# Long convolutions of a hybrid encoder layer: two stages of a 16-point transform as sums inside the matrix products

## The chip, the cores and the metric

One core of a Trainium2 chip runs the whole layer as one program. The metric is the device time of that program in microseconds (us); lower is better. Before the change three runs gave 3840.48, 3847.14 and 3849.62 us, median 3847.14 us.

## The reference, cut to what matters

The layer has four token mixers side by side. The one that the change touches is the Hyena mixer, two long convolutions over 2048 tokens in 256 channels:

```
def fft_long_conv(u, h_freq, skip):
    l = u.shape[1]
    uf = jnp.fft.rfft(u, n=2 * l, axis=1)
    y = jnp.fft.irfft(uf * h_freq[None], n=2 * l, axis=1)[:, :l]
    return y + u * skip

def hyena_mixer(z, ...):
    v, x1, x2 = jnp.split(short_conv(z, ...), 3, axis=-1)
    y = x1 * fft_long_conv(v, hf[:, 0], s[0])
    y = x2 * fft_long_conv(y, hf[:, 1], s[1])
```

Beside it stand a state space mixer and two softmax attentions with four heads each; then an output projection, a feed-forward part and a gated embedding. All is float32.

## The kernel before, in words

**The convolution.** Each long convolution is computed by `long_conv` (L1210) for half of the channels (128) at a time: two halves `hh`, two orders, so four calls, one after the other. The 2048 tokens are 128 rows (partitions) by 16 time residues t. A transform over the tokens is a 128-point part, done as matrix products with the tables `c_dft_f` and `c_dft_i`, and a 16-point part over t, done as two rounds of 4-point transforms with element-wise instructions. A 4-point transform (`Dft16.four`) is `first` (two instructions over 128x512: sums and differences, L1022 and L1023) and `last` (two over 128x256 and four over 128x128, L1028 to L1033). `rotate` multiplies by twiddle factors (nine ScalarE copies with a scale and one addition).

One call goes through three stages:

- Forward: for b = 0 to 3, two groups (a) of four products of 128 columns each into one PSUM tile (L1221), one ScalarE copy of it into `h_z` (L1223), then `four` from `h_z` over `h_s` back to `h_z`, then `rotate`.
- Middle: for ka = 0 to 3, `four`, the product with the filter's spectrum `h_sp`, the inverse `four`, `rotate`. No TensorE work.
- Inverse: for b = 0 to 3, the inverse `four` from `h_s` over `h_z` back to `h_s`, then eight products of 128 columns (L1255) into one PSUM tile, then one VectorE product with the gate (L1258).

The instructions of b (or ka) = 0 and 2 run on GpSimd (POOL), those of 1 and 3 on VectorE (DVE), by the list `ENG[1]`.

**What runs beside it.** `hyena_main` is a background generator: `Background.advance` is called once for each of the twelve steps of an attention unit (64 units, one for each head and 128 queries) and takes from the generator as many pieces as its costs (the numbers in `yield`) allow. So the four calls lie inside the attention, whose units need TensorE for scores (L447), transposes (L491) and weighted sums (L501), VectorE for moving each score block out of PSUM (L450, L452), ScalarE for exponentials (L457) and for moving transposes out (L496). The next generator in the queue forms the operands of the output projection (`out_weights`), in memory that the convolutions have left. The final order on each engine is written by a planner that simulates the program; the priority of background pieces is raised by 150 instructions. Each engine then takes its list in order.

Of the kernel before, what the change touches and what calls it, by code (L numbers as in the profile page):

```python
# [11 lines left out]
F32 = mybir.dt.float32  # L12
# [3 lines left out]
AF = mybir.ActivationFunctionType  # L16
# [1183 lines left out]
def hyena_main(ops, const, A, S, cp, wk, ps_pool):  # L1200

    tc, nc = ops.tc, ops.nc
    dft = Dft16(ops, wk, 128, [nc.vector if e else nc.gpsimd for e in ENG[1]])

    def mats(src, which):
        f = wk.tile([128, 2, 2, 128], F32, name="h_mat", bufs=4)
        nc.sync.dma_start(f, src[:, which, 0:2])
        return f

    def long_conv(u, order, hh, gate, dst):  # L1210
        z = wk.tile([128, 2, 16, 128], F32, name="h_z", bufs=1)
        s = wk.tile([128, 2, 16, 128], F32, name="h_s", bufs=1)
        for b in range(4):
            eng = dft.engines[b]
            zc, sc = z[:, :, b::4], s[:, :, b::4]
            for a in range(2):
                f = mats(A["c_dft_f"], slice(b + 4 * a, None, 8))
                ps = ps_pool.tile([128, 512], F32, name="ps_hy", tag="ps_hy").rearrange("p (t r c) -> p t r c", t=2, r=2)
                for i in range(2):
                    for r in range(2):  # L1220
                        nc.tensor.matmul(ps[:, i, r], lhsT=f[:, i, r], rhs=u[:, b + 4 * a + 8 * i], start=i + r == 0,  # L1221
                                         stop=True, skip_group_check=True)
                nc.scalar.activation(zc[:, :, a::2].rearrange("p r t c -> p t r c"), ps, AF.Copy)  # L1223
                yield 1.7
            yield from dft.four(eng, zc, sc, False)
            if b:
                dft.rotate(eng, zc, sc, b, False)
                yield 1.6
        for ka in range(4):
            eng = dft.engines[ka]  # L1230
            zc, sc = z[:, :, ts(ka, 4)], s[:, :, ts(ka, 4)]
            sp = wk.tile([128, 2, 4, 128], F32, name="h_sp", bufs=2)
            nc.sync.dma_start(sp, S["hspec"][order, hh, :, ka])
            yield from dft.four(eng, zc, sc, False)
            for r in range(2):
                eng.tensor_tensor(sc[:, r], zc[:, r], sp[:, 0], ALU.mult)
            for r in range(2):
                eng.tensor_tensor(zc[:, r], zc[:, r], sp[:, 1], ALU.mult)
            yield 2.2
            eng.tensor_tensor(sc[:, 0], sc[:, 0], zc[:, 1], ALU.subtract)  # L1240
            eng.tensor_tensor(sc[:, 1], sc[:, 1], zc[:, 0], ALU.add)
            yield 1.1
            yield from dft.four(eng, sc, zc, True)
            if ka:
                dft.rotate(eng, sc, zc, ka, True)
                yield 1.6
        for b in range(4):
            zc, sc = z[:, :, b::4], s[:, :, b::4]
            yield from dft.four(dft.engines[b], sc, zc, True)
            ps = ps_pool.tile([128, 4, 128], F32, name="ps_hy", tag="ps_hy")  # L1250
            for a in range(2):
                f = mats(A["c_dft_i"], slice(b + 8 * a, b + 8 * a + 5, 4))
                for i in range(2):
                    for r in range(2):
                        nc.tensor.matmul(ps[:, 2 * a + i], lhsT=f[:, i, r], rhs=sc[:, r, 2 * a + i],  # L1255
                                         start=a + i + r == 0, stop=r == 1, skip_group_check=True)
                yield 1.7
            nc.vector.tensor_mul(dst[:, b::4], ps, gate[:, b::4])  # L1258
            yield 0.6

    for hh in range(2):
        v, x1, x2 = (wk.tile([128, 16, 128], F32, name=n, bufs=1) for n in ("hy_v", "hy_x1", "hy_x2"))
        for j, d in enumerate((v, x1, x2)):
            nc.sync.dma_start(d, S["hyc"][2 * j + hh])
        yield from long_conv(v, 0, hh, x1, v)
        yield from long_conv(v, 1, hh, x2, x1)
        nc.sync.dma_start(S["yhs"].rearrange("(p t) c -> p t c", t=16)[:, :, ts(hh, 128)], x1)
        yield 0.0

# [374 lines left out]
C, S, T, W = "combine", "scale", "transpose", "weigh"  # L1644
# [39 lines left out]
def tile_hybrid_encoder(ctx, tc, A, out):  # L1684
# [28 lines left out]
    with ExitStack() as ac:  # L1713
# [21 lines left out]
        bg.add(together(background(s5_setup, "ss_c", "ss_w", "right"), hyena_conv, "hc_c", "hc_w", EMN[1]))  # L1735
        bg.add(together(background(s5_main, "sm_c", "sm_w", "right"), embedding, "em_c", "em_w", EMN[0]))
        bg.add(background(hyena_main, "hm_c", "hm_w", "right"))
        bg.add(out_weights)
        ip.run(const, bg.advance, lambda: bg.until(4))
# [100 lines left out]
```

## Time and profile before

| | |
|---|---|
| median of three runs | 3847.14 us |
| the profiled execution's own time | 3846.66 us |
| its span in the profile | 3844.9 us |
| mean granted TensorE clock | 0.953 of full |
| attention, first to last score or sum | 558.8 to about 1996 us |
| the four long convolutions | 1310 to 1882 us |

The span is the time from the first to the last instruction of the profiled execution; times of rows below count from its start. Engines are PE (TensorE products), PEld (TensorE weight loads, beside PE), DVE (VectorE), ACT (ScalarE), POOL (GpSimd), SP (which issues DMAs). "Busy" is the time in which an engine had at least one instruction in execution; for PE the ends are modelled and consecutive products overlap.

### The profile page before, as it was taken

The numbers are of one execution on the slowest core, as the hardware profiler recorded it, in microseconds if no ns is written. First come the engines' busy times: TensorE is split into PE (matmuls) and PEld (weight loads), VectorE is DVE, ScalarE is ACT, GpSimd is POOL, SyncE is SP. The second block draws the span as 40 slices with busy tenths as digits, with TensorE's granted clock in tenths as the row PEclk, the third lists the DMA queues.
The fourth block names the chain that finished last, engine by engine and source line by source line (L and its number), as shares of the span: only waits on it lengthen the run. The fifth ranks groups of instructions, "written<-read, shape, count | busy, mean of one in ns | idle before, by whom it ended". The sixth has DMA issues, their size and how long they took to land. (4 is left out here: it accounts for less than half of the span.)

```text
span 3844.9 us, 55782 instructions
## 1 busy us (share of the span) xinstructions
PE 3504.9 (91%) x19814; PEld 2782.5 (72%) x19814; DVE 2678.9 (70%) x5382; ACT 1802.5 (47%) x3089; POOL 1869.3 (49%) x1735
## 2 busy tenths in 40 slices
PE   8999988998999977877889979999999998989887
PEld 6889876676777756665667768887788876767666
DVE  6657538777565698798767774447554577777877
ACT  5334316666666655655664443334333343333344
POOL 1333003671663587677546554445444444344454
PEclk9999999999999988988899989999999999999998
DMA  4544652226223412421244452223322244445644
GB/s 145 181 142 162 221 164 50 104 90 194 91 93 98 153 37 83 121 56 55 85 160 154 149 164 77 88 78 99 102 88 79 85 162 168 172 153 170 210 165 151
DMA packets 350998, 480.45 MB, mean 125 GB/s; under 512 B 57307, under 2 KB 257759, under 8 KB 346207
## 3 DMA queue, kind: packets, MB, share of 16 engines
q1 hardware_dynamic: 276672, 369.13, 31.0%
q10 hardware_dynamic: 74048, 107.76, 7.9%
q8 instruction: 156, 2.56, 0.3%
q14 instruction: 122, 1.00, 0.1%
HBM read 313.46 MB, written 167.53 MB: 125 GB/s over the span
## 5 line engine op out<-in xcount | busy, mean ns | idle before, releaser
L447 PE MATMUL ps_s<-k_sb,q_sb 96*128 96x512 f32 x1280 | 483.9, 466 | 109.9 <-DVE four_s L452 51.1
L457 ACT ACTIVATE at_s<-at_s,least_s 128x2048 f32<-128x2048 f32 x192 | 383.8, 2000 | 133.1 <-DVE least_s L456 127.5
L817 PE MATMUL ps_st<-t_hi,s_hi 128*128 128x512 f32 x984 | 398.5, 406 | 49.3 <-DVE st_sum L844 24.0
L452 DVE CUSTOM_DVE_ANT_0 at_s<-ps_s,strip 128x512 f32<-128x512 f32 x512 | 340.1, 684 | 126.1 <-PE ps_s L447 102.4
L817 PE MATMUL ps_st<-t_lo,s_hi 128*128 128x512 f32 x984 | 395.4, 402 | 17.0 <-DVE t_lo L41 17.0
L496 ACT ACTIVATE at<-ps_at 128x512 f32<-128x512 f32 x512 | 292.0, 593 | 231.9 <-PE ps_at L491 197.6
L817 PE MATMUL ps_st<-t_hi,s_lo 128*128 128x512 f32 x984 | 393.8, 401 | 5.6 <-DVE s_lo L41 5.6
L447 PEld LDWEIGHTS ps_s<-k_sb,q_sb 96*128 96x128 f32 x1280 | 233.8, 202 | 206.6 <-DVE four_s L452 77.9
L40 ACT ACTIVATE s_hi<-s_raw 128x512 fp32r<-128x512 f32 (+1 forms) x336 | 207.4, 618 | 357.9 <-PE ps_st L817 283.3
L501 PE MATMUL ps_o<-at,v_sb 128*64 128x128 f32 x4096 | 352.9, 296 | 11.2 <-DVE o_sb L518 4.8
L491 PE MATMUL ps_at<-ident,at_s 128*128 128x128 f32 x2048 | 325.5, 293 | 39.4 <-ACT at L496 23.9
L41 DVE TENSOR_TENSOR s_lo<-s_raw,s_hi 128x512 fp32r<-128x512 f32 (+1 forms) x336 | 265.8, 793 | 133.4 <-ACT s_hi L40 133.2
L501 PEld LDWEIGHTS ps_o<-at,v_sb 128*64 128x64 f32 x4096 | 256.8, 145 | 111.5 <-issue 91.7
L40 ACT ACTIVATE a_hi<-a_raw 128x512 fp32r<-128x512 f32 (+1 forms) x252 | 155.2, 618 | 379.8 <-PE ps_st L817 212.4
L491 PEld LDWEIGHTS ps_at<-ident,at_s 128*128 128x128 f32 x2048 | 258.5, 150 | 100.5 <-ACT at L496 33.0
L801 POOL TENSOR_TENSOR s_raw<-a_raw 128x512 f32<-128x512 f32 (+1 forms) x84 | 113.6, 1352 | 441.1 <-DMA a_raw<-in_w_up_dram 136.1
L817 PE MATMUL ps_st<-b_hi,a_hi 128*128 128x512 f32 x656 | 263.1, 401 | 34.8 <-ACT b_hi L40 15.6
L41 DVE TENSOR_TENSOR a_lo<-a_raw,a_hi 128x512 fp32r<-128x512 f32 (+1 forms) x252 | 232.5, 924 | 76.0 <-ACT a_hi L40 75.0
L471 POOL TENSOR_SCALAR at_s<-at_s,f 128x1024 f32<-128x1024 f32 (+1 forms) x48 | 74.7, 1556 | 424.1 <-DMA q_sb<-d_qmr 193.0
L817 PEld LDWEIGHTS ps_st<-t_hi,s_hi 128*128 128x128 f32 x984 | 191.5, 195 | 102.1 <-DVE st_sum L844 28.3
L817 PE MATMUL ps_st<-b_lo,a_hi 128*128 128x512 f32 x656 | 260.8, 398 | 4.5 <-DVE b_lo L41 3.1
L817 PE MATMUL ps_st<-b_hi,a_lo 128*128 128x512 f32 x656 | 259.4, 396 | 0.0
(521 smaller groups left out, 8883.1 us busy)
## 6 DMA issues: line engine op xcount, KB each, us to landing
d_h<-st_row ACTq DMA_DIRECT2D x64, 512.0 KB, 3.3
st_row<-d_h SPq DMA_DIRECT2D x64, 512.0 KB, 4.4
a_raw<-in_w_gate_dram SPq DMA_DIRECT2D x44, 512.0 KB, 4.1
a_raw<-in_w_up_dram SPq DMA_DIRECT2D x44, 512.0 KB, 3.9
d_g<-st_row ACTq DMA_DIRECT2D x44, 512.0 KB, 3.9
f_mat<-in_c_dft_f_dram SPq DMA_DIRECT2D x32, 512.0 KB, 4.1
a_raw<-d_g SPq DMA_DIRECT2D x32, 512.0 KB, 4.9
w_raw<-in_w_in_dram SPq DMA_DIRECT2D x48, 256.0 KB, 3.4
```

What stands on the lines that cost most here:

```text
L40: nc.scalar.activation(hi, src, AF.Copy)
L41: nc.vector.tensor_sub(lo, src, hi.bitcast(F32))
L447: nc.tensor.matmul(ps, lhsT=lhs, rhs=rhs[:, ts(c, 512)], start=n == 0, stop=n == len(products) - 1)
L452: nc.vector.tensor_tensor_reduce(dst, ps, at.strip[:, ds(1920 - 128 * self.t + 512 * c, 512)], self.slope, 3e38, ALU.add, ALU.min, least)
L457: nc.scalar.activation(s, s, AF.Exp, bias=least, scale=-1.0, accum_out=self.total[name])
L471: nc.gpsimd.tensor_scalar(s2[:, n:], s2[:, n:], f, 0.0, ALU.mult, ALU.add)
L491: nc.tensor.transpose(ps[:, j], src[:, ts(4 * g + j, 128)], at.ident)
L496: nc.scalar.activation(tile, ps, AF.Copy)
L501: mm = lambda out, lhsT, rhs, first, last: nc.tensor.matmul(out, lhsT=lhsT, rhs=rhs, start=first, stop=last, skip_group_check=True)
L801: eng.tensor_add(s1, a21, a22)
L817: nc.tensor.matmul(bank, lhsT=l[x][:, c], rhs=r[y], start=first and c + k == 0, stop=c == kb - 1 and k == 2, skip_group_check=True)
```

## The change

In the forward stage `first` goes away. Its sums and differences of the parts t and t + 8 are made in PSUM: for each table the product with u[t] is written to both halves of the tile (a broadcast operand, 256 columns), and the product with u[t + 8] and with its negative (256 columns, from a tile that holds u[8:16] a second time with its sign turned, at index 16 to 23) is added. The ScalarE copy puts the tile into `h_s` and `last` follows.

In the inverse stage `last` goes away. `first` stays; a ScalarE copy makes the negatives of the odd parts, and each of the four outputs of the 4-point transform is accumulated from two operands for each table: sixteen products of 128 columns in place of eight.

The negated copy of the input is made by ScalarE: once for each half of the channels over 128x1024, and in the first order's inverse stage once for each b over 128x256. The input tile `hy_v` grows from 16 to 24 parts, and the costs in `yield` change.

```diff
-                for i in range(2):
-                    for r in range(2):
-                        nc.tensor.matmul(ps[:, i, r], lhsT=f[:, i, r], rhs=u[:, b + 4 * a + 8 * i], start=i + r == 0,
-                                         stop=True, skip_group_check=True)
-                nc.scalar.activation(zc[:, :, a::2].rearrange("p r t c -> p t r c"), ps, AF.Copy)
-                yield 1.7
-            yield from dft.four(eng, zc, sc, False)
+                for r in range(2):
+                    mm(ps[:, :, r], lhsT=f[:, 0, r], rhs=u[:, t][:, None, :].to_broadcast([128, 2, 128]), start=r == 0,
+                       stop=False, skip_group_check=True)
+                    mm(ps[:, :, r], lhsT=f[:, 1, r], rhs=u[:, t + 8 :: 8], start=False, stop=True, skip_group_check=True)
+                nc.scalar.activation(sc[:, :, a::2].rearrange("p r t c -> p t r c"), ps, AF.Copy)
+                yield 2.4
+            dft.last(eng, zc, sc, False)
+            yield 2.2
...
-            yield from dft.four(dft.engines[b], sc, zc, True)
+            dft.first(dft.engines[b], zc, sc[:, :, 0:2], sc[:, :, 2:4])
+            neg = sc[:, :, 0:2]
+            nc.scalar.activation(neg, zc[:, :, 1::2], AF.Copy, scale=-1.0)
+            yield 2.2
+            re, im, rn, jn = zc[:, 0], zc[:, 1], neg[:, 0], neg[:, 1]
+            terms = (((re[:, 0], re[:, 1]), (im[:, 0], im[:, 1])), ((re[:, 2], jn[:, 1]), (im[:, 2], re[:, 3])),
+                     ((re[:, 0], rn[:, 0]), (im[:, 0], jn[:, 0])), ((re[:, 2], im[:, 3]), (im[:, 2], rn[:, 1])))
...
-                        nc.tensor.matmul(ps[:, 2 * a + i], lhsT=f[:, i, r], rhs=sc[:, r, 2 * a + i],
-                                         start=a + i + r == 0, stop=r == 1, skip_group_check=True)
-                yield 1.7
-            nc.vector.tensor_mul(dst[:, b::4], ps, gate[:, b::4])
+                        for k, x in enumerate(terms[2 * a + i][r]):
+                            mm(ps[:, 2 * a + i], lhsT=f[:, i, r], rhs=x, start=a + i + r + k == 0, stop=r + k == 2,
+                               skip_group_check=True)
+                yield 2.4
+            nc.vector.tensor_mul(dst[:, b:16:4], ps, gate[:, b:16:4])
+            if again:
+                nc.scalar.activation(dst[:, 16 + b :: 4], dst[:, 8 + b : 16 : 4], AF.Copy, scale=-1.0)
             yield 0.6
...
-            nc.sync.dma_start(d, S["hyc"][2 * j + hh])
-        yield from long_conv(v, 0, hh, x1, v)
-        yield from long_conv(v, 1, hh, x2, x1)
+            nc.sync.dma_start(d[:, 0:16], S["hyc"][2 * j + hh])
+        nc.scalar.activation(v[:, 16:24], v[:, 8:16], AF.Copy, scale=-1.0)
+        yield from long_conv(v, 0, hh, x1, v, True)
+        yield from long_conv(v, 1, hh, x2, x1, False)
```

## Rows read from the trace of the kernel before

**Rows 1.** The page: busy time of each engine over the span.

```profile
PE 3504.9 (91%) x19814; PEld 2782.5 (72%) x19814; DVE 2678.9 (70%) x5382; ACT 1802.5 (47%) x3089; POOL 1869.3 (49%) x1735
```

**Rows 2.** Windows by stage: stretch, length, busy time of engines, clock, DMA share, GB/s.

```profile
1324.00:1350.00 26.00, 24.64 (x209) 19.63 (x208) 20.88 (x53) 21.60 (x46) 22.70 (x24) 1.00 0.39 119
1350.00:1420.00 70.00, 48.38 (x286) 34.78 (x285) 69.79 (x134) 31.84 (x61) 60.26 (x55) 0.75 0.12 40
1420.00:1452.00 32.00, 29.80 (x229) 23.48 (x229) 27.57 (x64) 19.37 (x35) 22.61 (x22) 0.96 0.23 67
1452.00:1480.00 28.00, 25.75 (x202) 20.96 (x197) 19.62 (x57) 19.16 (x42) 22.99 (x25) 0.95 0.45 139
1480.00:1552.00 72.00, 51.68 (x348) 38.59 (x347) 68.52 (x134) 35.31 (x69) 55.99 (x54) 0.78 0.13 40
1552.00:1590.00 38.00, 35.07 (x254) 27.20 (x254) 31.45 (x77) 20.20 (x33) 25.05 (x24) 0.96 0.19 55
1590.00:1622.00 32.00, 29.31 (x244) 23.63 (x243) 24.72 (x63) 24.72 (x46) 21.03 (x22) 1.00 0.86 246
1622.00:1696.00 74.00, 52.14 (x316) 37.39 (x317) 70.41 (x132) 32.66 (x62) 58.75 (x54) 0.74 0.27 70
1696.00:1735.00 39.00, 37.09 (x307) 30.49 (x307) 35.22 (x94) 25.71 (x49) 26.49 (x28) 0.96 0.21 62
1735.00:1766.00 31.00, 31.00 (x264) 24.96 (x264) 23.72 (x71) 23.78 (x40) 19.78 (x18) 1.00 0.32 95
1766.00:1846.00 80.00, 54.83 (x347) 38.86 (x348) 75.17 (x150) 41.70 (x90) 71.34 (x70) 0.79 0.08 23
1846.00:1881.00 35.00, 31.87 (x251) 25.77 (x247) 29.40 (x70) 16.28 (x24) 16.98 (x16) 0.95 0.14 42
```

**Rows 3.** Windows: attention before and after the convolutions, same columns.

```profile
550.00:1310.00 760.00, 707.05 (x5105) 522.54 (x5104) 520.60 (x1421) 489.18 (x698) 371.78 (x428) 0.96 0.36 109
1885.00:2000.00 115.00, 100.01 (x800) 75.20 (x796) 78.11 (x205) 77.72 (x115) 55.65 (x55) 0.90 0.40 133
```

**Rows 4.** Groups, a middle stage (1766 to 1846): busy, mean ns | idle before, releasers.

```profile
L447 PE MATMUL ps_s<-k_sb,q_sb 96*128 96x512 f32 x61 | 27.3, 529 | 21.4 <-DVE four_s L452 13.9 <-DVE at_s L450 6.6 <-DMA q_sb<-d_qda 0.8
```

**Rows 5.** Groups, a forward stage (1735 to 1766), the same line.

```profile
L447 PE MATMUL ps_s<-k_sb,q_sb 96*128 96x512 f32 x36 | 12.8, 438 | 0.0
```

**Rows 6.** Tile h_mat: the convolutions' products, duration ns min/median/max, first and last start.

```profile
L1221 PE MATMUL ps_hy<-hy_v,h_mat x256: 272/275/377, 1324.1 to 1762.3; 128*128 128x128 f32 x128
L1255 PE MATMUL ps_hy<-h_s,h_mat x256: 272/275/582, 1431.8 to 1878.0; 128*128 128x128 f32 x128
```

**Rows 7.** Timeline of weight loads at 1335: start us, length us, count.

```profile
1334.90 1.86 PEld L1221 LDWEIGHTS ps_hy<-hy_v,h_mat 128*128 128x128 f32 x16
```

**Rows 8.** Timeline of PE at 1158: products of 256 columns.

```profile
1157.94 1.03 PE L1574 MATMUL ps_hy<-s5m_m,s5m_uT 128*128 128x256 f32 x4
1158.81 0.38 PE L1577 MATMUL ps_hy<-s5m_wout,s5m_xs 128*128 128x256 f32 x1
```

**Rows 9.** Groups of 1324 to 1880: VectorE and GpSimd instructions of the 4-point transforms.

```profile
L1022 DVE TENSOR_TENSOR h_s<-h_z 128x512 f32<-128x512 f32 x16 | 23.8, 1487 | 1.8 <-POOL h_s L1023 1.6
L1023 DVE TENSOR_TENSOR h_s<-h_z 128x512 f32<-128x512 f32 x16 | 19.2, 1199 | 0.0
L1028 DVE TENSOR_TENSOR h_s<-h_z 128x256 f32<-128x256 f32 x16 | 13.2, 824 | 0.0
L1033 DVE TENSOR_TENSOR h_s<-h_z 128x128 f32<-128x128 f32 x16 | 9.5, 595 | 0.0
L1022 POOL TENSOR_TENSOR h_s<-h_z 128x512 f32<-128x512 f32 x16 | 21.8, 1365 | 19.0 <-ACT h_z L1223 11.9 <-DVE h_z L1028 4.1 <-DVE h_z L1053 3.0
L1028 POOL TENSOR_TENSOR h_s<-h_z 128x256 f32<-128x256 f32 x16 | 17.2, 1074 | 0.2
```

**Rows 10.** Groups of 1324 to 1880: ScalarE copies of the convolutions.

```profile
L1223 ACT ACTIVATE h_z<-ps_hy 128x512 f32<-128x512 f32 x32 | 18.8, 593 | 14.2 <-PE ps_hy L1221 14.2
L1050 ACT ACTIVATE h_s<-h_z 128x256 f32<-128x256 f32 x36 | 13.6, 416 | 11.3 <-DVE h_z L1031 9.9 <-DVE h_z L1033 1.2
```

**Rows 11.** Groups of 1324 to 1880: the inverse stage's products.

```profile
L1255 PE MATMUL ps_hy<-h_s,h_mat 128*128 128x128 f32 x256 | 39.0, 289 | 5.2 <-DVE h_s L1032 3.8 <-DVE h_s L1028 1.4
```

More of the change, by code (lines that the diff above doesn't have):

```diff
@@ L1208, in mats, with long_conv @@
         return f
-    def long_conv(u, order, hh, gate, dst):
+    def long_conv(u, order, hh, gate, dst, again):
         z = wk.tile([128, 2, 16, 128], F32, name="h_z", bufs=1)
         s = wk.tile([128, 2, 16, 128], F32, name="h_s", bufs=1)
+        mm = nc.tensor.matmul
         for b in range(4):
@@ L1216, in long_conv @@
             for a in range(2):
-                f = mats(A["c_dft_f"], slice(b + 4 * a, None, 8))
+                t = b + 4 * a
+                f = mats(A["c_dft_f"], slice(t, None, 8))
                 ps = ps_pool.tile([128, 512], F32, name="ps_hy", tag="ps_hy").rearrange("p (t r c) -> p t r c", t=2, r=2)
-                for i in range(2):
-                    for r in range(2):
-                        nc.tensor.matmul(ps[:, i, r], lhsT=f[:, i, r], rhs=u[:, b + 4 * a + 8 * i], start=i + r == 0,
-                                         stop=True, skip_group_check=True)
-                nc.scalar.activation(zc[:, :, a::2].rearrange("p r t c -> p t r c"), ps, AF.Copy)
-                yield 1.7
-            yield from dft.four(eng, zc, sc, False)
+                for r in range(2):
[6 more added lines that the diff above has]
+            yield 2.2
             if b:
@@ L1254, in long_conv @@
                     for r in range(2):
-                        nc.tensor.matmul(ps[:, 2 * a + i], lhsT=f[:, i, r], rhs=sc[:, r, 2 * a + i],
-                                         start=a + i + r == 0, stop=r == 1, skip_group_check=True)
-                yield 1.7
-            nc.vector.tensor_mul(dst[:, b::4], ps, gate[:, b::4])
+                        for k, x in enumerate(terms[2 * a + i][r]):
[5 more added lines that the diff above has]
+                nc.scalar.activation(dst[:, 16 + b :: 4], dst[:, 8 + b : 16 : 4], AF.Copy, scale=-1.0)
             yield 0.6
     for hh in range(2):
-        v, x1, x2 = (wk.tile([128, 16, 128], F32, name=n, bufs=1) for n in ("hy_v", "hy_x1", "hy_x2"))
+        v, x1, x2 = (wk.tile([128, n, 128], F32, name=name, bufs=1) for name, n in (("hy_v", 24), ("hy_x1", 16), ("hy_x2", 16)))
         for j, d in enumerate((v, x1, x2)):
-            nc.sync.dma_start(d, S["hyc"][2 * j + hh])
-        yield from long_conv(v, 0, hh, x1, v)
-        yield from long_conv(v, 1, hh, x2, x1)
+            nc.sync.dma_start(d[:, 0:16], S["hyc"][2 * j + hh])
+        nc.scalar.activation(v[:, 16:24], v[:, 8:16], AF.Copy, scale=-1.0)
+        yield from long_conv(v, 0, hh, x1, v, True)
+        yield from long_conv(v, 1, hh, x2, x1, False)
         nc.sync.dma_start(S["yhs"].rearrange("(p t) c -> p t c", t=16)[:, :, ts(hh, 128)], x1)
```

## The prediction

> **What bounds the kernel now.** The page's first part puts TensorE ahead of all engines over the whole span, 91% busy against 70% for VectorE [rows 1]. That mean says nothing about the convolutions, so I went from the timeline of one call (which shows where its three stages lie) to the windows, one for each stage of each of the four calls [rows 2]. The reader is to see two kinds of row. The four middle stages (the windows of 70, 72, 74 and 80 us, 296 us together) have VectorE at 94 to 100% and TensorE at 69 to 72% with a clock of 0.74 to 0.79. The eight forward and inverse stages (26, 32, 28, 38, 32, 39, 31 and 35 us, 261 us together) have TensorE at 91 to 100% with a clock of 0.95 or more: its busy times add up to 244.5 us of 261, so 16.5 us are idle. VectorE has 212.6 us there (81%), ScalarE 170.8 (65%), GpSimd 177.6 (68%).
>
> The groups say the same by what ends the waits. In the last middle stage the score products waited 21.4 us, 20.5 of them for VectorE to empty a PSUM tile [rows 4]; in the forward stage just ahead of it, 0.0 us [rows 5]. So the limit changes from stage to stage, and the change takes VectorE and GpSimd work out of, and puts TensorE work into, the stages in which TensorE is the limit.
>
> **The change part by part.**
>
> Forward products. Each call has 32 products of 128 columns, four calls 128; the trace has 256 records of them [rows 6], so a product is two passes. Sixteen passes started within 1.86 us [rows 7], 116 ns each. Passes of 256 columns stand elsewhere in the trace: four began in 0.87 us (1157.94 to 1158.81) [rows 8], 217 ns each. The number of products stays 128, each now with 256 columns: 256 passes x (217 - 116) = +25.9 us of TensorE.
>
> Inverse products. Sixteen for each b in place of eight, again 128 columns: 128 more products, 256 more passes (as many as there are now, [rows 6]) x 116 ns = +29.7 us. Together +55.6 us of TensorE time, all in the eight stages with 16.5 us of TensorE idle. The floor under the cost is that every idle microsecond there is filled: 55.6 - 16.5 = +39.1. If the idle share stays as it is (244.5 of 261), the cost is 55.6 / 0.937 = +59.3. I take the floor, +39, because one of the eight windows already runs with no idle at all (31.00 of 31.00, [rows 2]).
>
> The work does not have to stay in these stages: where the planner lets the convolutions go first, it is the attention's products that are pushed out. Then they land in the middle stages, which VectorE closes, or behind the convolutions, where TensorE is 87% busy (100.0 of 115, [rows 3]) and where a unit's work must still be done. So the place changes, the cost hardly.
>
> `first` of the forward stage: two VectorE instructions for b = 1 and 3, so 8 of the 16 of each line (the other 8 belong to the middle stage): (23.8 + 19.2) / 2 = 21.5 us [rows 9]. `last` of the inverse stage: half of six groups, from 13.2 to 9.5 us, 62.6 together, so 31.3 us ([rows 9] shows the first and the last of the six). VectorE loses 52.8 us and GpSimd a like amount (half of 21.8 and so on, about 56). In these stages VectorE falls from 81% to some 61%. I count nothing for it: what TensorE waited for there is already inside the 16.5 us. That includes the 5.2 us in which inverse products waited for `last` [rows 11]; the new last step ahead of them is the ScalarE negation. If VectorE and not TensorE were the cover, it would be worth up to its 52.8 us, which is the case of the first rival.
>
> ScalarE. Added are 16 negations of 128x512, bounded by 416 ns for 256 elements from SBUF and 593 ns for 512 from PSUM [rows 10], so about 0.6 us each, 9.5 us; 8 copies of 128x256, 3.3 us; two of 128x1024, about 1.2 us each by twice the 512 row. Together 15 us, beside an engine that is 65% busy there: nothing on the path; 15 us if it were all in the chain. Each also adds a wait, and ScalarE takes its list in order: behind a negation that waits for `first` stand exponentials and the copies that empty transposes, for which TensorE then waits. The nearest row is the twiddle copies that wait for the same kind of instruction, 11.3 us over 36 of them [rows 10], so 5 us for 16; upper bound, all on the path, +5; I take 0. The two 128x1024 copies wait for a DMA, which the planner can place behind its landing; 0, at most some us.
>
> Order and memory. The costs of a call fall from 122.8 to 116.4 (eight times 0.8 less), so the next generator enters the list about 26 steps, or two attention units, sooner; its memory is that of the convolutions, so it still cannot begin before they end. The DMAs are the same in number and size. The planner writes a new order for all that follows; a shift of 10 us either way from that alone is my guess, with no row behind it, and it widens the range.
>
> Sum: 3846.66 (the profiled execution's own time, 1.8 us over its span and 0.5 us under the median) + 25.9 + 29.7 - 16.5 = 3885.8, so **3886 us**. Its own range, from the idle share kept to ten us of luck: 3865 to 3912.
>
> A rule speaks against this reading. The Trainium skill ("Perfetto Trace Analysis", section "Identifying the Most-Contended Engine") holds that the busy share of products is a poor measure of TensorE's headroom, since they overlap, and that the share of weight loads is the better one. By that rule the eight stages have room: loads are 196.1 us of 261, 75%. This case's trace bears it out only in part: the busiest of the eight windows has loads at 81% (24.96 of 31) and no idle product time. By loads alone the 55.6 us would fit into 65 us that are left, which is the first rival's condition.
>
> **The rivals.**
>
> Faster: TensorE's busy time hides slack, the extra passes go into it, and the convolutions' chain is what paces these stages. For it: GpSimd waits 19.0 us in front of `first` [rows 9], the stages are also 81% full on VectorE, and every b loses two to six instructions of its chain. Against it: score products wait 0.0 us in a forward stage [rows 5]. Price: if the whole stretch of 557 us stays 89% full on VectorE (496.5 us of rows 2) and that work falls by 52.8, it is 498 us, 59 less; TensorE at 100% allows 451.6 + 55.6 = 507, 50 less: 3797. With half of it, 3822. It decides where TensorE has more than 55.6 us of unused issue time in the 261 us.
>
> Nothing: the two effects meet, for example with the extra passes fitting into some 40 us of slack and the negations costing the rest: 3840 to 3858.
>
> Slower by more: the idle share stays (+59) and the negations' waits land on the path, with up to 15 us of ScalarE work: 3846.7 + 59 + 15 = 3921. For it: in the 760 us before the convolutions, also TensorE-bound, TensorE is not above 93% either [rows 3].
>
> **How the numbers follow.** Forecast with its own range 0.56, slower by more (above 3912) 0.10, nothing 0.12, faster 0.22. A measurement of this kernel tells about 0.3% (11.5 us) from no change. Faster by more than that is the faster rival, 0.22; within it 0.12; slower the rest, 0.66. The range goes from 3824, which leaves out the full gain of the faster rival, to 3916, leaving out most of the heavy one: about 0.2 outside.
>
> **What would show it.** Forward passes of about 217 ns spacing and 256 records as before; 512 inverse records at 116 ns. The forward and inverse windows longer by about 39 us together, or fewer attention units done in them, with TensorE at 97% or more and VectorE near 60%; the middle windows as before, VectorE at 95% or more; the end of the attention near 2035 instead of 1996. The prediction is wrong if these windows keep their length and their share of attention with 55 us more passes in them, if the middle stages get shorter, or if score products start to wait for VectorE less while the end comes earlier.

## The result, and the profile after

The change makes the kernel slower. Median 3906.39 us against 3848.38, ratio 1.0132 with a 95% interval of 1.0112 to 1.0152, so 43 to 58 us; the two medians by themselves would give 1.0151, the upper end of that interval. Timed again on another chip the ratio was 1.0145 (1.0127 to 1.0164). The forecast was 3886 us, with a range of 3824 to 3916; the measured time lies in it, and in the narrower range of the forecast alone, 3865 to 3912.

The profiled execution took 3895.67 us, its span is 3893.9 us, 49.0 more than the span before. Two rows place it. Line 518 is the last VectorE instruction of each attention unit; its columns are the shortest, median and longest duration in ns, then the first and the last start. Before:

```profile
L518 DVE TENSOR_TENSOR o_sb<-ps_o,o_sb x64: 264/281/293, 602.7 to 1995.2; 128x128 f32<-128x128 f32 x64
```

After:

```profile
L518 DVE TENSOR_TENSOR o_sb<-ps_o,o_sb x64: 265/285/293, 602.1 to 2036.3; 128x128 f32<-128x128 f32 x64
```

The attention, first to last of these, went from 1392.5 to 1434.2 us, +41.7. What lies behind it (span less last start) went from 1849.7 to 1857.6, +7.9; what lies ahead of it is 0.6 us shorter. All comparisons below use these two lengths beside the total. The attention's length can be cut once more, into the time in which TensorE is busy and the time in which it is idle. The columns are those of [rows 2], over the attention, first before, then after:

```profile
602.70:1995.20 1392.50, 1233.82 (x9072) 926.45 (x9070) 1068.14 (x2635) 869.39 (x1391) 847.71 (x880) 0.92 0.30 94
602.10:2036.30 1434.20, 1284.79 (x9312) 966.23 (x9310) 1038.79 (x2570) 883.53 (x1415) 791.39 (x817) 0.93 0.29 92
```

TensorE is busy for 51.0 us more (1233.8 to 1284.8) and idle for 9.3 us less (158.7 to 149.4).

The page after, busy time by engine (answers to [rows 1]): TensorE +57.4 us, VectorE -17.5, GpSimd -40.3. The last two understate what was removed, since outside the attention, where the code is the same, both engines were busy longer: in the attention alone VectorE is busy for 29.3 us less (1068.1 to 1038.8) and GpSimd for 56.3 less (847.7 to 791.4). About 53 and 56 us were taken out.

```profile
PE 3562.3 (91%) x20070; PEld 2831.2 (73%) x20070; DVE 2661.4 (68%) x5318; ACT 1818.6 (47%) x3115; POOL 1829.0 (47%) x1671
```

The windows by stage after, drawn near the same points of each call as in [rows 2] (to some us), same columns (PE, PEld, DVE, ACT, POOL, clock, DMA share, GB/s):

```profile
1320.00:1350.00 30.00, 29.77 (x171) 22.93 (x172) 16.58 (x53) 22.45 (x47) 16.59 (x21) 1.00 0.38 122
1350.00:1422.00 72.00, 48.12 (x327) 36.85 (x325) 68.31 (x130) 33.69 (x66) 57.79 (x54) 0.76 0.12 37
1422.00:1450.00 28.00, 28.00 (x238) 24.34 (x239) 17.54 (x38) 15.15 (x28) 13.57 (x9) 1.00 0.25 73
1450.00:1481.00 31.00, 31.00 (x195) 24.09 (x195) 16.67 (x48) 20.48 (x44) 14.52 (x18) 1.00 0.38 121
1481.00:1552.00 71.00, 45.31 (x290) 32.78 (x286) 67.55 (x127) 31.79 (x58) 56.95 (x54) 0.74 0.14 42
1552.00:1598.00 46.00, 46.00 (x346) 36.51 (x344) 27.95 (x76) 28.38 (x51) 15.36 (x12) 1.00 0.17 51
1598.00:1641.00 43.00, 43.00 (x297) 32.42 (x296) 25.65 (x75) 26.58 (x53) 20.03 (x22) 1.00 0.54 164
1641.00:1710.00 69.00, 49.19 (x293) 33.39 (x292) 62.63 (x122) 31.68 (x63) 57.70 (x54) 0.74 0.34 87
1710.00:1766.00 56.00, 56.00 (x454) 46.94 (x453) 37.38 (x109) 36.56 (x62) 22.95 (x17) 0.96 0.16 48
1766.00:1810.00 44.00, 43.80 (x312) 33.57 (x312) 24.87 (x73) 29.00 (x56) 18.64 (x22) 1.00 0.22 65
1810.00:1881.00 71.00, 46.77 (x296) 33.60 (x292) 67.64 (x132) 31.31 (x62) 57.28 (x54) 0.74 0.07 23
1881.00:1940.00 59.00, 56.92 (x454) 45.12 (x453) 39.26 (x98) 35.44 (x59) 26.60 (x20) 0.99 0.12 33
```

Add up the eight forward and inverse windows: 337 us, TensorE busy 334.5 of them (99%, before 94%), VectorE 205.9 (61%, before 81%). The four middle windows: 283 us, TensorE 189.4 (67%), VectorE 91 to 95%. So the stages kept their limits. TensorE's idle time fell from 16.5 to 2.5 us in the eight windows, and rose from 89.0 to 93.6 us in the four middle ones. The lengths alone mislead, since attention work moved between the stages: the eight windows hold 304 records of score products (before 245), the four middle ones 183 (before 222); a record on a border counts in both windows.

Where the score products waited, after: the first row is a forward stage (1766 to 1810), the second a middle stage (1810 to 1881); they answer to [rows 5] and [rows 4]. Nothing in the one, 15.9 us in the other, all but 0.1 for VectorE.

```profile
L447 PE MATMUL ps_s<-k_sb,q_sb 96*128 96x512 f32 x40 | 14.7, 448 | 0.0
...
L447 PE MATMUL ps_s<-k_sb,q_sb 96*128 96x512 f32 x44 | 19.2, 516 | 15.9 <-DVE at_s L450 8.6 <-DVE four_s L452 7.2
```

The products themselves after, by tile (answers to [rows 6]), the new forward ones in the second and third row: 256 forward records and 512 inverse ones.

```profile
L1269 PE MATMUL ps_hy<-h_z,h_mat x384: 272/275/377, 1424.6 to 1938.6; 128*128 128x128 f32 x192
L1225 PE MATMUL ps_hy<-hy_v,h_mat x128: 377/379/484, 1321.5 to 1805.2; 128*128 128x256 f32 x128
L1227 PE MATMUL ps_hy<-hy_v,h_mat x128: 377/379/382, 1322.1 to 1805.6; 128*128 128x256 f32 x128
L1269 PE MATMUL ps_hy<-h_s,h_mat x128: 272/275/377, 1428.7 to 1938.8; 128*128 128x128 f32 x128
```

Three starts of the forward ones in the timeline after (start, duration; answers to [rows 8]): 0.43 us from one pair of 256-column passes to the next, 215 ns a pass.

```profile
1322.07 0.59 PE L1227 MATMUL ps_hy<-hy_v,h_mat 128*128 128x256 f32 x2
1322.50 0.59 PE L1225 MATMUL ps_hy<-hy_v,h_mat 128*128 128x256 f32 x2
1322.93 0.59 PE L1227 MATMUL ps_hy<-hy_v,h_mat 128*128 128x256 f32 x2
```

### The profile page after: what moved, and what is told of

The parts are those of the page before. It is cut to its first block, busy times and chain, and to the rows that moved or that the text cites. A ratio compares the mean times of both kernels' runs of the same rounds, so it can differ in the third digit from the quotient of the medians.

```text
span 3893.9 us, 56210 instructions
## 1 busy us (share of the span) xinstructions
PE 3562.3 (91%) x20070; PEld 2831.2 (73%) x20070; DVE 2661.4 (68%) x5318; ACT 1818.6 (47%) x3115; POOL 1829.0 (47%) x1671
## 5 line engine op out<-in xcount | busy, mean ns | idle before, releaser
L501 PE MATMUL ps_o<-at,v_sb 128*64 128x128 f32 x4096 | 363.1, 296 | 7.5 <-DVE o_sb L518 5.2
```

Source lines behind the costliest of these rows:

```text
L501: mm = lambda out, lhsT, rhs, first, last: nc.tensor.matmul(out, lhsT=lhsT, rhs=rhs, start=first, stop=last, skip_group_check=True)
```

## The experiments

Ratios are against the kernel before on the same chip, with 95% intervals; the difference is the ratio less 1, times 3848 us. The last two columns are one profiled execution each: the attention, and what lies behind it, as changes against 1392.5 and 1849.7 us. They do not add up to the total: the stretch ahead of the attention differs by up to 7 us, and the kernel before has one profile only, so an error in it is in every row.

| run | ratio (interval) | total, us | attention | behind |
|---|---|---|---|---|
| the change | 1.0132 (1.0112 to 1.0152) | +51 | +41.7 | +7.9 |
| a2_again | 1.0145 (1.0127 to 1.0164) | +56 | +46.2 | +9.0 |
| e1_forward | 1.0035 (1.0020 to 1.0051) | +13 | +21.7 | -5.4 |
| e2_inverse | 1.0069 (1.0052 to 1.0086) | +27 | +23.0 | +8.2 |
| e3_double | 1.0207 (1.0189 to 1.0225) | +80 | +54.7 | +24.3 |
| e4_less_vector | 0.9950 (0.9935 to 0.9965) | -19 | -23.6 | +5.3 |
| e5_old_costs | 1.0111 (1.0093 to 1.0129) | +43 | +38.8 | +7.9 |
| e6_both | 1.0091 (1.0075 to 1.0108) | +35 | +27.0 | +5.0 |
| e7_no_negation | 1.0066 (1.0050 to 1.0082) | +25 | +36.5 | -11.8 |
| e9_no_copies | 1.0124 (1.0108 to 1.0140) | +48 | +39.1 | +9.6 |
| e8_middle | 0.9915 (0.9897 to 0.9933) | -33 | -42.3 | +4.9 |
| e10_middle_all | 1.0010 (1.0000 to 1.0021) | +4 | -44.6 | +52.8 |

**The same kernel again.**

> The changed kernel once more, for its interval on this chip and a second profile: about +51 us over before, and in the profile the attention (first to last L518) again near 1434 us and the stretch behind it near 1858 us, if both are set by the order of the program; if the 8 us behind the attention were chance of one execution, near 1850.

The attention was 4.5 us longer than in the first profile, what lies behind it 1.1 us. So about 5 us is what one profile's attention tells from another's, and the 8 to 9 us behind the attention repeat in this program, as far as two profiles against one can tell. The idle time of TensorE in the attention repeated too, 149.7 us; nearly all of the 4.5 us is busy time, +55.2 in place of +51.0:

```profile
605.20:2043.90 1438.70, 1289.01 (x9317) 969.04 (x9315) 1038.90 (x2571) 883.89 (x1416) 792.42 (x818) 0.93 0.29 91
```

**Half of the change at a time.** e1 keeps the old inverse, e2 the old forward stage.

> Only the forward stage as in the change (256-column products, no first sums and differences, negated copy of the input); the inverse stage as before. Passes theory (the change costs what its added TensorE passes cost in stages where TensorE is the limit, and the removed vector work is worth nothing): 256 passes 101 ns longer, +26 us, so +20 to +32 us over before. Waits theory (the loss comes from the new ScalarE negations in front of the inverse products): near 0, -5 to +8. Vector theory (removed VectorE and GpSimd work is worth its time and hides part of the cost): 26 minus some 10 to 20, +5 to +15.

> Only the inverse stage as in the change (sixteen products for each b, a ScalarE negation, no last step); the forward stage as before. Passes theory: 256 passes of 116 ns, +30 us, +23 to +37. Waits theory: nearly the whole loss of the change, +45 to +60. Vector theory: 30 minus the worth of the removed last steps (31 us of VectorE), -5 to +15.

In the attention the two halves cost 21.7 and 23.0 us, together 44.7, as the whole does (41.7 and 46.2). Each costs a little less than its passes, 25.9 and 29.7. The loss is not in the inverse stage alone, so the waits theory falls. By the totals the other two are not told apart: e2, +27, lies in the range of the passes theory, but e1, +13, lies in that of the vector theory. By the attention both halves fit the passes. The two readings of e1 differ by 9 us because one is of single executions: its profiled one was 3.5 us above its median (3869.58 against 3866.10), and that of the kernel before 5.8 us below the median it is compared with here (3846.66 against 3852.42). Inside the profile the stretch behind the attention, 5.4 us shorter, and the one ahead of it, 6.4 us longer, nearly cancel.

**The passes without the rest.**

```diff
-                        nc.tensor.matmul(ps[:, i, r], lhsT=f[:, i, r], rhs=u[:, b + 4 * a + 8 * i], start=i + r == 0,
-                                         stop=True, skip_group_check=True)
+                        for k in range(2):
+                            nc.tensor.matmul(ps[:, i, r], lhsT=f[:, i, r], rhs=u[:, b + 4 * a + 8 * i], start=i + r + k == 0,
+                                             stop=k == 1, skip_group_check=True)
```

and likewise in the inverse stage; the copies out multiply by 0.5.

> The kernel before with every forward and inverse product of the long convolutions issued twice into the same sums, halved when the sum is read out; all vector work stays, no negations. 512 more passes of 116 ns, +59 us of TensorE, 4 us more than the change adds. Passes theory: +50 to +65 us, about the change's own loss. Waits theory: the passes are hidden, 0 to +20. Vector theory: the loss of the change plus what the removed vector work is worth, +75 or more.

The attention grew by 54.7 us for 512 passes of 116 ns, 59.4 us: 0.92 of a microsecond for each microsecond of passes, or 0.84 to 1.0 with the 5 us of one profile. TensorE was busy for 57.0 us more in it, and idle for only 2.3 less (156.4 in place of 158.7):

```profile
604.50:2051.70 1447.20, 1290.81 (x9579) 981.39 (x9577) 1058.37 (x2623) 863.39 (x1382) 833.12 (x872) 0.93 0.28 87
```

The other 24 us are another thing. First line: the attention's last unit. Second: the forming of the output projection's weights, which waits for the convolutions' memory.

```profile
L518 DVE TENSOR_TENSOR o_sb<-ps_o,o_sb x64: 265/284/297, 604.5 to 2051.7; 128x128 f32<-128x128 f32 x64
...
L589 POOL TENSOR_SCALAR b_raw<-b_raw,op_g x16: 688/692/2171, 2027.1 to 2085.6; 128x512 f32<-128x512 f32 x16
```

The convolutions ended so late (the last stores issued at 2015.4) that the last of this work began 34 us after the attention's end; in the change it began 22 us ahead of it (2014.7 against 2036.3). That this is where the 24 us come from is read from the order of the two, not tested by itself. So the total of e3 overstates the passes, and the attention is the better measure. By the total the vector theory's range would be met (+75 or more), by the attention the one of the passes theory (+50 to +65).

**The removed vector work without the passes.**

```diff
-                nc.scalar.activation(zc[:, :, a::2].rearrange("p r t c -> p t r c"), ps, AF.Copy)
-            yield from dft.four(eng, zc, sc, False)
+                nc.scalar.activation(sc[:, :, a::2].rearrange("p r t c -> p t r c"), ps, AF.Copy)
+            dft.last(eng, zc, sc, False)
...
-            yield from dft.four(dft.engines[b], sc, zc, True)
+            dft.first(dft.engines[b], zc, sc[:, :, 0:2], sc[:, :, 2:4])
```

> The kernel before without the first step of the forward stage and without the last step of the inverse stage, and nothing in their place (their sums and differences are left out), the costs for the planner as before. It takes away the 53 us of VectorE and about 56 us of GpSimd that the change takes away and adds no product. Passes theory: nothing gained, -8 to +3 us. Vector theory: -20 to -50 us. Waits theory: says nothing of it, about 0.

-23.6 us in the attention, -19 in total: the removed work, 53 us of VectorE and about as much of GpSimd, is worth something, although no product was taken away. The passes theory in its strict form ("nothing gained") misses here, and the vector theory is at the edge of its numbers.

> Every product of the forward and inverse stages twice, and the first step of the forward and the last step of the inverse stage left out (their sums are missing): 59 us of passes added, 53 us of VectorE and 56 us of GpSimd removed, no negations, old costs. If the two effects seen so far add up (+80 for the passes, -19 for the vector work): +52 to +70 us, near the change's own +51. If removed vector work is worth nothing once TensorE is the limit: +72 to +85.

With the doubled products in place as well, leaving the vector work out still saved 27.7 us of attention (+27.0 against +54.7). The total, +35, is below both expectations. TensorE's idle time in the attention fell by 21.6 us (137.0 in place of 158.7), against 2.3 in e3:

```profile
608.60:2028.10 1419.50, 1282.45 (x9579) 978.52 (x9577) 1023.61 (x2561) 866.73 (x1386) 786.53 (x812) 0.93 0.29 90
```

So in this form the vector work is worth 24 to 28 us of attention whether the passes are there or not.

**Pace, negations, copies.** In e5 the pace is the one of the kernel before, in the forward stage as here and likewise in the inverse one:

```diff
-                yield 2.4
+                yield 1.7
+            yield 2.2
```

> The change, with costs for the background generator that add up to those of the kernel before (122.8 for a call in place of 116.4), so that the pieces are asked for at the old pace. Passes theory: the loss stays, +45 to +60 us over before. Order theory (a good part of the loss comes from the new pace and the planner's new order): +20 to +35.

Most of the loss stays (+43 in total, just under the passes theory's range; +38.8 in the attention, 3 to 7 us under the change's two profiles). So the pace is not a good part of it, and the order theory, as far as it is about the pace, falls; a few us of it remain possible.

> The change without the sixteen ScalarE negations of the inverse stage; the products read the operand with its sign unturned (so those signs are left wrong). Passes theory: the negations cost nothing, +43 to +58 us over before as the change. Waits theory: their waits are 10 us or more of the loss, +40 or less.

```diff
-            neg = sc[:, :, 0:2]
-            nc.scalar.activation(neg, zc[:, :, 1::2], AF.Copy, scale=-1.0)
+            neg = zc[:, :, 1::2]
```

By the total the waits theory would win (+25). By the place it does not: the attention is 5 to 10 us shorter than in the change, and 20 us of the difference lie behind the attention, in the output projection, which has no negation. All twelve programs have the same code there; without e3 and e10, where the weights come late, its length runs from 1837.9 (e7) to 1859.3 us (e9), and it repeated within 1.1 us when one program ran twice. So I put it down to the order that the planner writes for it; that was not tested by itself.

e9 leaves out the second negation and the copies of the input tile too (the forward products then read the same columns twice):

```diff
-            if again:
-                nc.scalar.activation(dst[:, 16 + b :: 4], dst[:, 8 + b : 16 : 4], AF.Copy, scale=-1.0)
...
-        nc.scalar.activation(v[:, 16:24], v[:, 8:16], AF.Copy, scale=-1.0)
```

> The change without any negated copy: neither the sixteen negations of the inverse stage nor the ten copies of the input's second half; the products read the operands with their sign unturned (those signs are left wrong). Same passes as the change, same removed vector work. Copies theory (the vector work is worth some 25 us in the attention, and the new ScalarE copies give most of it back by their place in the chain from stage to stage): attention near 1392 + 51 - 25 = 1418 us, total +20 to +35. Passes theory as forecast (the removed vector work and the copies are both worth nothing): attention 1430 us or more, total +43 or more. In between (1424 to 1430), the form of the forward products has a share.

1431.6 us in the attention: this is in the range of the passes theory, and the copies are not what eats the saving. All 26 ScalarE instructions together cost 3 to 7 us of attention, which two profiles of one kernel can just show.

**The same move in the other stage.** e8 is the kernel before with the first step of the middle stage's 4-point transforms (ka = 1 and 3, VectorE's) made by TensorE:

```diff
+        for w in (const["ident"], minus):
+            ps = ps_pool.tile([128, 2, 2, 128], F32, name="ps_hy", tag="ps_hy")
+            nc.tensor.matmul(ps, lhsT=const["ident"], rhs=z[:, :, 0:2], start=True, stop=False)
+            nc.tensor.matmul(ps, lhsT=w, rhs=z[:, :, 2:4], start=False, stop=True)
+            t.append(ps)
...
+        nc.scalar.activation(s[:, :, 1], lo[:, :, 1], AF.Copy)
+        nc.scalar.activation(s[:, :, 3], hi[:, :, 1], AF.Copy)
+        tt(z[:, :, 0], lo[:, :, 0], s[:, :, 1], ALU.add)
...
```

> The kernel before, with the same kind of move put into the middle stages, where VectorE is the limit and TensorE was idle for some 89 of 296 us: for ka = 1 and 3 the sums and differences of both 4-point transforms' first step are made by products with the identity and its negative (64 products of 512 columns, two passes each, about 55 us of TensorE), ScalarE copies the odd halves out (32 of 128x256, 13 us), VectorE loses its 41 us of first steps. If what counts is which engine limits the stage: -10 to -30 us. If added TensorE passes cost their time wherever they stand: +10 to +55.

3816.68 us, 33 us faster than before (0.9915, interval 0.9897 to 0.9933), a little more than expected, with about as many microseconds of passes added as the change adds. It beats both kernels. Windows of e8 over the first call's forward and middle stage, then over all four calls:

```profile
1320.00:1350.00 30.00, 29.73 (x246) 22.70 (x246) 24.43 (x57) 23.53 (x48) 24.69 (x25) 1.00 0.41 132
1350.00:1412.00 62.00, 48.38 (x289) 31.46 (x290) 55.69 (x114) 31.44 (x62) 51.96 (x54) 0.89 0.15 45
...
1320.00:1860.00 540.00, 488.99 (x3518) 356.35 (x3519) 449.28 (x1096) 333.31 (x642) 413.84 (x408) 0.95 0.27 76
```

The middle stage took 62 us in place of 70, with the same 48.38 us of TensorE busy in it, at a granted clock of 0.89 in place of 0.75 [rows 2]. Two things changed together there, the waits of TensorE and its clock. First the waits. Columns: waiting line, releaser, us in total, times, longest. In e8 the score products waited 34.9 us for VectorE over the four calls,

```profile
PE ps_s L447 <- DVE four_s L452: 18.1, 7, 10.1
PE ps_s L447 <- DVE at_s L450: 16.8, 13, 2.9
```

before, 68.0 us, and in the changed kernel 63.6 us; the first two lines are of the kernel before, the last two of the changed one:

```profile
PE ps_s L447 <- DVE four_s L452: 41.9, 19, 7.4
PE ps_s L447 <- DVE at_s L450: 26.1, 19, 5.2
...
PE ps_s L447 <- DVE four_s L452: 41.7, 20, 6.7
PE ps_s L447 <- DVE at_s L450: 21.9, 12, 4.2
```

Then the clock. The granted clock is a mean over stretches at full and at half speed (2.4 and 1.2 GHz). In the first middle stage a record of a score product took 573 ns on average before, at 0.75, and 478 ns in e8, at 0.89; the third line is e8's attention:

```profile
L447 PE MATMUL ps_s<-k_sb,q_sb 96*128 96x512 f32 x54 | 25.5, 573 | 16.9 <-DVE four_s L452 8.8 <-DVE at_s L450 8.0
...
L447 PE MATMUL ps_s<-k_sb,q_sb 96*128 96x512 f32 x47 | 17.9, 478 | 11.8 <-DVE four_s L452 11.2 <-DVE at_s L450 0.6
...
604.30:1954.50 1350.20, 1247.76 (x9209) 920.95 (x9207) 1017.21 (x2604) 877.12 (x1425) 833.82 (x882) 0.96 0.31 97
```

TensorE was idle for 56.2 us less in the attention (102.4 in place of 158.7), and busy for only 13.9 more, though some 55 us of passes were added (an estimate: 128 passes of 512 columns, each taken at twice the 215 ns of 256 columns): at a mean clock of 0.96 in place of 0.92 the same work took less time. So the gain of 42 us is shorter waits and a higher clock together. The higher clock came with the fuller TensorE; no run separates the two.

e10 does it for all four ka; for the two of GpSimd, ScalarE copies the sums out first:

```diff
-        if eng is nc.gpsimd:
-            yield from dft.four(eng, z, s, inv)
-            return
...
+        if eng is nc.gpsimd:
+            nc.scalar.activation(s[:, :, 0:2], lo, AF.Copy)
+            nc.scalar.activation(s[:, :, 2:4], hi, AF.Copy)
+            dft.last(eng, z, s, inv)
+            yield 2.2
+            return
```

> The kernel before with the first steps of the middle stage on TensorE for all four ka; for the two of GpSimd, ScalarE copies both tiles out (32 more copies of 128x512, 19 us), and some 55 us of passes come on top of those of ka = 1 and 3. If VectorE and GpSimd together still limit the middle stages: 10 to 20 us faster than with ka = 1 and 3 alone, -40 to -52 under before. If TensorE is then the limit there (its idle time was 89 us, the passes are 110): no better than ka = 1 and 3 alone, -30 to 0.

The attention gained no more than in e8 (-44.6 against -42.3), and the total went back to that of before. Now TensorE is the limit in the middle stages too. The four calls as one window of e10, then two stretches inside middle stages, then the attention:

```profile
1320.00:1940.00 620.00, 594.37 (x4205) 416.75 (x4204) 443.59 (x1237) 405.85 (x748) 382.43 (x392) 0.99 0.23 69
...
1400.00:1450.00 50.00, 48.12 (x332) 32.58 (x332) 33.48 (x94) 34.83 (x66) 29.12 (x31) 1.00 0.12 35
1640.00:1720.00 80.00, 76.67 (x506) 50.82 (x508) 51.63 (x153) 53.31 (x98) 45.95 (x47) 0.98 0.12 37
...
603.60:1951.50 1347.90, 1283.31 (x9299) 928.24 (x9297) 936.31 (x2567) 880.49 (x1431) 751.11 (x820) 0.98 0.28 89
```

And its waits of TensorE there, of the same two lines:

```profile
PE ps_s L447 <- DVE at_s L450: 3.3, 3, 2.8
PE ps_s L447 <- DVE four_s L452: 2.6, 4, 1.3
```

TensorE is 96% busy over the four calls and its score products wait 5.9 us for VectorE. The convolutions end at 1948 us, in e8 at 1855, the forming of the weights falls behind the attention (last at 2019.5, attention's last unit at 1951.5), and what lies behind the attention is 52.8 us longer than before. The total is a little worse than the numbers expected for a TensorE limit, since they did not include this.

## Why the prediction was right, and where its sizes were off

**The limit of each stage.** Right. The eight stages in which work was added ran at 99% of TensorE after; the waits of score products for VectorE lie nearly all in the middle stages and hardly changed (68.0 us before, 63.6 after). e8 and e10 confirm it from the other side: the same kind of move gains where VectorE is the limit, until TensorE is the limit there too.

One of the prediction's own signs of being wrong did come: the middle windows are shorter, 283 us in place of 296, with VectorE at 91 to 95% in place of 95% or more. They hold less attention work (183 records of score products in place of 222), and VectorE is busy for 17.8 us less in them (283.9 to 266.1). The length of a window told where the attention's work had been placed and not what limits the stage, so the sign was badly chosen; why less of it was placed there was not tested.

**The passes and the idle time.** The counts were right (256 and 512 records), and so was the spacing of the forward passes (215 ns for 217). The sum took +55.6 us for the passes and -16.5 for idle time that they fill. In the attention TensorE is busy for 51.0 and 55.2 us more in the two profiles of the change, so the first term held. The second was too large: the idle time fell by 9 us, not 16.5. In the eight stages it fell by 14.0, nearly as forecast, but in the middle stages, which the sum left alone, it rose by 4.6. And the passes by themselves filled less: in e3, where all vector work stays, the idle time of the attention fell by 2.3 us, and 0.92 us were paid for each microsecond of passes, 51 us for 55.6. By that reading the cost of the passes, taken at the floor of 39, was mis-sized by 12 us, inside its bounds of 39 and 59.

**The vector work, counted at nothing.** Wrong as a term: e4 and e6 against e3 put it at 24 to 28 us in the attention. In the change itself less of it arrives: 51 us of passes less 42 to 46 leaves 5 to 9, and 12 in e9, where no copy stands in the way; each of these is a difference of single profiles, good to some 5 us. What takes the remaining 12 to 16 us between e6 and e9 is open: they differ in the form of the forward products (128 of 256 columns against 256 of 128), in the place and size of the input tile, in the pace, and through all of these in the planner's order. The two wrong terms lean against each other: idle time counted as filled by the passes alone, and vector work counted at nothing although it is what lets idle time be filled (21.6 us in e6, 2.3 in e3). That 39 came near the attention's 42 to 46 is in part luck.

**The negations and copies, counted at nothing.** 3 to 7 us of attention (e9 against the change's two profiles), at the edge of what can be seen.

**Order behind the attention.** The forecast had a guess of 10 us either way for it; it came out at +8 to +9 against the one profile of before. With the +41.7 of the attention and -0.6 ahead of it the 49.0 us of the first profiled execution are complete. The forecast named 2035 us for the attention's end; it was 2036.3 and 2043.9.

So the mechanism holds: work added where TensorE is the limit costs nearly its whole time. The total is larger than forecast, 51 or 56 us against 39, because the stretch behind the attention was not in the sum and because the floor was taken for the passes; the vector work that was left out of the sum took back part of that. What the planner's order adds behind the attention stays unexplained.

The rule that the share of weight loads measures TensorE's room better than that of products (the Trainium skill, "Perfetto Trace Analysis", section "Identifying the Most-Contended Engine") would have allowed 65 us in the eight stages. That section of the Trainium skill names the rate of arithmetic beside the loads; it was not worked out here. The stages filled up at loads of 79% (265.9 us of 337) with products at 99%: here the loads came to 87% in the fullest window (24.34 of 28), and the products' busy share told where the room ended.

## What to carry to other kernels

Before moving work from one engine to another, cut the time into the stages in which the work stands and ask which engine's waits end last in each: the same kind of move cost 51 us in two stages of this loop and gained 33 us in the one between them. A relieved engine that is not the limit can still be worth a part of its time, so test that term alone (leave the work out) instead of setting it to zero. Cut a measured length into the limiting engine's busy and idle time: that showed which term of the sum was off. And when a planner orders the program, compare the stretches that the edit cannot touch as well: here they moved by up to 20 us between kernels and nearly gave one experiment the wrong winner.

## What the runs showed that was not expected

The end of a background task can cost more than its work: in e3 and e10 the convolutions ended later, the next task in their memory was no longer covered by the attention, and 24 and 53 us appeared in a stage that the edit does not touch (two runs agree; moving that task alone was not tried). And the granted TensorE clock of a middle stage rose from 0.75 to 0.89 when products were put into it and TensorE was busy for 78% of the stage in place of 69%; over the attention it went from 0.92 to 0.96 in e8 and 0.98 in e10, and some 55 us of added passes made TensorE busy for only 14 us longer in e8.
